# One gated DeltaNet layer on one core: instruction order from a timeline model, with the last products in written order

## The chip, the cores and the metric

The kernel runs on one core of one Trainium2 chip. The metric is device time in microseconds (us) of one execution. The time before is the median of three executions; one more execution was profiled, and all rows of the trace below come from that one.

## The reference: what is computed

One decoder layer: adaptive RMSNorm, the gated DeltaNet mixer (16 value heads, 8 key/query heads, head size 128, 1024 tokens), an output projection, a gated residual sum and a last RMSNorm. Cut to what matters:

```python
hdn = rms_norm(x, norm_g) * (1 + scale) + shift            # 1024 x 1024
qkv, z, b, a = split(hdn @ w_in)                           # 32 + 16 column tiles of 128, and 32 columns
q, k, v = split(silu(causal_depthwise_conv(qkv, conv_w)))  # 4 taps
T = inverse(I + strict_lower(beta * k k^T * decay))        # per chunk and head, a triangular solve
for chunk in chunks:                                       # state S per head
    r = v - (k * e^g) S ;  u = T (beta * r)
    o = (q * e^g) S + (q k^T * decay) u ;  S = S * e^g_last + k_dec^T u
o = rms_norm(o) * silu(z)
out = rms_norm(x + gate * (o @ w_out), final_g)
```

## The kernel before

All matrix products run in fp32 split in two parts (`hi` and `lo`); a product is three matmuls: hi·hi, hi·lo, lo·hi. The two value heads that share a key head form a group, so there are eight groups. After a start-up part (lines 357 to 419: x is normalised, turned and modulated) the middle part (lines 928 to 964) runs the groups as a software pipeline. While group g is scanned over its 8 chunks (`scan`, L677), group g+1 is prepared:

- `norms` (L487) builds the decay mask `em`: 16 DVE instructions (L497), then one Exp on ACT over 2048 columns (L499).
- `stage_a` (L534) makes the matrices of the triangular solve, and solves 32x32 blocks on DVE: 31 dependent pairs of instructions, a multiply (L575) and a subtract (L577), here called the solve. The result goes to DRAM and back (L579, then eight loads at L596), is transposed on DVE (L597 to L599) and is merged by TensorE (`levels`, L587, first matmuls L603 and L605).
- `values` (L632) and `proj_kq` (L474) make projections: 24 matmuls of 512 columns each (L459), a copy and a scaling on ACT (L442, L444), three tap additions on DVE (L446), Silu on ACT (L447), then for values a transpose on TensorE (L639). Their weights come by DMA (L139) into three raw buffers, and are split by ACT (L123) and POOL (L124).
- `out_gate` (L667) makes the gate z; `residual_gate` (L781) runs once, beside group 1's scan, and works on DVE at L229.

TensorE's order in the middle part is written out by hand: `drive` (L902) interleaves the generators by costs and delays in ns, such as `D_L0` = 46000, after which a group's `levels` are placed. `early` (L861) starts the output projection (heads 0 to 3) as filler beside the last two groups.

The end (lines 966 to 1013) computes the other output products, heads 4 to 15, in two halves of tokens (`tg`), each with eight PSUM accumulators of 512 columns: first a loop over heads 4 to 12, then for each of four row tiles the heads 13 to 15, the residual sum on DVE (L847, L848), the sum of squares on ACT (L1012) and `finish` (L986: power on POOL, scaling, store).

What sets the order: the program is traced in written order and then ordered by a scheduler of the framework, which replays it on a model of the machine. On each engine, and on the queue of SP that issues nearly all DMAs, it puts next the instruction that is first in written order among those that are ready at that moment of the model. Every engine then runs its list strictly in that order, waiting where an input isn't there yet. Inside a `tc.manual_schedule(engines=...)` block, the named engines keep the written order instead. Before the change, TensorE is named in the middle part, four engines in most of the start-up part, and DVE alone in the last loop of the end.

Of the kernel before, what the change touches and what calls it, by code (L numbers as in the profile page):

```python
# [17 lines left out]
P = 128  # L18
EPS = 1e-6
# [14 lines left out]
EARLY, NLAST = 4, 3  # L34
# [13 lines left out]
def gdn_layer(ctx: ExitStack, tc: tile.TileContext, x, c, ada_w, ada_b, norm_g, w_in, conv_w, a_log, dt_bias,  # L48
# [8 lines left out]
    nc = tc.nc  # L57
    B, T, D = x.shape
# [3 lines left out]
    HV = 16  # L62
    NTAP = conv_w.shape[1]
    TH = 512
# [17 lines left out]
    neg_half = const.tile([P, 8], F32, name="neg_half")  # L82
# [39 lines left out]
    def split(raw, hi, lo):  # L122
        nc.scalar.copy(hi, raw)  # L123
        nc.gpsimd.tensor_tensor(lo, raw, hi.bitcast(F32), op=ALU.subtract)  # L124
# [27 lines left out]
    banks = ["pj", "pj", "ks", "oq", "ts", "pot"]  # L152

    def bank(tag, shape=(P, TH)):
        return pp.tile(list(shape), F32, name=tag, tag=tag, bufs=nbuf.get(tag, 1))
# [267 lines left out]
    cp = ctx.enter_context(tc.tile_pool(name="cp", bufs=2))  # L423
# [253 lines left out]
    def scan(gi, G):  # L677
# [47 lines left out]
        for n in range(NT):  # L725
# [4 lines left out]
            while len(late) > LAG:  # L730
                if can_finish():
                    finish(*late.pop(0))
                yield 0, 400
            pks = bank("ks", (P, 2, 2, P))
            if n > 0:
                nc.tensor.matmul(pks[:, 0], lhsT=kq[:, 0, js], rhs=st, start=True, stop=True)  # L736
                r = cp.tile([P, 2, P], F32, name="r", tag="r", bufs=1)
                for h in range(2):
                    nc.vector.scalar_tensor_tensor(r[:, h], pks[:, 0, h], negc[:, n, h0 + h:h0 + h + 1], vtok[:, j, h],
                                                   op0=ALU.mult, op1=ALU.add)  # L740
                second(*pend)
                if len(late) > 2 and can_finish():
                    finish(*late.pop(0))
                if n < NT - 1:
                    sg = cp.tile([P, 2, P], F32, name="sg", tag="sg", bufs=1)
                    nc.gpsimd.tensor_tensor(sg, st, gle[:, n, hs, None].to_broadcast([P, 2, P]), op=ALU.mult)
                yield 860, D_R
            else:
                r = vtok[:, 0]
# [26 lines left out]
        while late:  # L776
            if can_finish():
                finish(*late.pop(0))
            yield 215, D_F
# [25 lines left out]
    def load_wo(kt, hf, hl):  # L805

        whi, wlo = hl
        raw = wpool.tile([P, TH], F32, name="woraw", tag="wraw", bufs=3)
        nc.sync.dma_start(out=raw, in_=w_out[kt * P:(kt + 1) * P, hf * TH:(hf + 1) * TH])
        nc.scalar.copy(whi, raw)  # L810
        (nc.vector if kt % 2 else nc.gpsimd).tensor_tensor(wlo, raw, whi.bitcast(F32), op=ALU.subtract)
        return whi, wlo

    def load_wo2(kt):
        hl = [wpool.tile([P, D], F32R, name=n, tag=t, bufs=2) for n, t in (("wohi", "whi"), ("wolo", "wlo"))]
        ww = []
        for hf in range(2):
            s = slice(hf * TH, (hf + 1) * TH)
            raw = wpool.tile([P, TH], F32, name="woraw", tag="wraw", bufs=3)
            nc.sync.dma_start(out=raw, in_=w_out[kt * P:(kt + 1) * P, s])  # L820
            split(raw, hl[0][:, s], hl[1][:, s])
            ww.append((hl[0][:, s], hl[1][:, s]))
        return ww

    def load_g(kt, tg, hl, pool=cp, tag="vT", bufs=2):
        src = pool.tile([P, TH], F32, name="gsrc", tag=tag, bufs=bufs)
        nc.sync.dma_start(out=src, in_=o_dram[kt, :, tg * TH:(tg + 1) * TH])
        ghi, glo = hl
        nc.scalar.copy(ghi, src)
        nc.vector.tensor_tensor(glo, src, ghi.bitcast(F32), op=ALU.subtract)  # L830
        return ghi, glo

    def out_product(acc, t, gw, ww, first, last):
        (ghi, glo), (whi, wlo) = gw, ww
        ts = slice(t * P, (t + 1) * P)
        for n, (a, b) in enumerate(((ghi, whi), (ghi, wlo), (glo, whi))):
            nc.tensor.matmul(acc, lhsT=a[:, ts], rhs=b, start=(first and n == 0), stop=(last and n == 2))  # L837

    wos, gos, rows32 = [], [], []
    rows_of = lambda tg, t: slice((tg * 4 + t) * P, (tg * 4 + t + 1) * P)  # L840
    xrs = {}
    running = []

    def gated_add(acc, yt, tg, t, hf):

        s = slice(hf * TH, (hf + 1) * TH)
        nc.vector.tensor_tensor(yt[:, s], acc, gate_b[:, s], op=ALU.mult)  # L847
        nc.vector.tensor_tensor(yt[:, s], yt[:, s], xrs[tg, t][:, s], op=ALU.add)  # L848
# [114 lines left out]
        for _ in tail:  # L963
            pass

    gate_b, fg = rows32[:2]
    nc.sync.dma_start(out=fg, in_=final_g[None, :].to_broadcast([P, D]))
    banks = ["pj", "pj", "tr", "tr", "ks", "oq", "ts", "pot"]
    last = range(HV - NLAST, HV)
    wlast = None  # L970
    for tg in range(2):
        acc = [[bank(banks[2 * t + hf]) for hf in range(2)] for t in range(4)]
        for kt in range(EARLY, HV - NLAST):
            ww = load_wo2(kt)
            gw = load_g(kt, tg, [cp.tile([P, TH], F32R, name=n, tag=t, bufs=b)
                                 for n, t, b in (("ghi", "ktok", 4), ("glo", "vtok", 3))])
            for t in range(4):
                for hf in range(2):
                    out_product(acc[t][hf], t, gw, ww[hf], kt == EARLY, False)
        if wlast is None:  # L980
            wos += [[cp.tile([P, TH], F32R, name=n, tag=t, bufs=b)
                        for n, t, b in (("wohi", "sz", 2), ("wolo", ("pn2", "tb")[hf], 1))] for hf in range(1)]
            wlast = [[load_wo(kt, hf, wos[2 * i + hf]) for hf in range(2)] for i, kt in enumerate(last)]
        glast = [load_g(kt, tg, gos[i]) for i, kt in enumerate(last)]

        def finish(rs, yt, ss, end):  # L986
            nc.vector.tensor_scalar(ss[:, 0:1], ss[:, 0:1], ss[:, 1:2], EPS, op0=ALU.add, op1=ALU.add)
            nc.gpsimd.tensor_tensor(ss[:, 0:1], ss[:, 0:1], neg_half[:, :1], op=ALU.pow)
            for hf in range(2):
                s = slice(hf * TH, (hf + 1) * TH)  # L990
                if end:
                    nc.vector.scalar_tensor_tensor(yt[:, s], yt[:, s], ss[:, 0:1], fg[:, s], op0=ALU.mult,
                                                   op1=ALU.mult)
                else:
                    nc.scalar.mul(yt[:, s], yt[:, s], ss[:, 0:1])
                    nc.gpsimd.tensor_tensor(yt[:, s], yt[:, s], fg[:, s], op=ALU.mult)
                nc.sync.dma_start(out=out[0, rs, s], in_=yt[:, s])

        with tc.manual_schedule(engines={nc.vector.engine}):
            for t in range(4):  # L1000
                if tg == 0:
                    yt = cp.tile([P, D], F32, name="yt", tag=("at", "at", "ua", "at")[t], bufs=(2, 2, 1, 2)[t])
                else:
                    yt = xrs[0, t]
                ss = cp.tile([P, 2], F32, name="ss", tag="ssk", bufs=2)
                xr = xrs[tg, t]
                for hf in range(2):
                    for i, kt in enumerate(last):
                        out_product(acc[t][hf], t, glast[i], wlast[i][hf], False, i == NLAST - 1)
                    gated_add(acc[t][hf], yt, tg, t, hf)  # L1010
                    s = slice(hf * TH, (hf + 1) * TH)
                    nc.scalar.activation(xr[:, s], yt[:, s], AF.Square, scale=D ** -0.5, accum_out=ss[:, hf:hf + 1])  # L1012
                finish(rows_of(tg, t), yt, ss, t == 3)


_INS = ["x", "c", "ada_w", "ada_b", "norm_g", "gdn_w_in", "gdn_conv_w", "gdn_a_log", "gdn_dt_bias", "gdn_norm_w",
# [19 lines left out]
```

## Time and profile before

| | us |
|---|---|
| median of three executions | 1133.0 (1131.27 to 1133.68) |
| the profiled execution, own time | 1130.95 |
| its span, first to last instruction | 1129.2 |
| TensorE busy in it (share of span) | 1059.3 (94%) |
| VectorE (DVE) | 745.1 (66%) |
| ScalarE (ACT) | 536.6 (48%) |
| GpSimd (POOL) | 450.0 (40%) |
| mean granted TensorE clock | 0.979 |

How to read it: the profiled execution is 2.05 us shorter than the median, and its span is 1.75 us shorter than its own time. A matmul's end in the trace is modelled, so TensorE's gaps are read rather than its busy time. Granted clock is a share of full speed: 1.00 is 2.4 GHz, 0.5 is 1.2 GHz.

### The profile page before, as it was taken

What the parts mean: (1) busy time and instruction counts of PE and PEld (TensorE: products, weight loads), DVE (VectorE), ACT (ScalarE), POOL (GpSimd) and SP (SyncE); (2) the same over time, 40 slices, a digit from 0 to 9 for tenths busy, and PEclk for the clock granted to TensorE, in tenths of its full rate; (3) what the DMA queues carried; (4) which work ended last, traced back from release to release, by engine and by line L of the source; (5) the groups of instructions that cost most, each with busy time, mean ns of one, the idle gap of its engine ahead of it and who ended that gap; (6) DMA issues with size and microseconds to landing.
All of it is one profiled execution on the core that took longest, in us unless ns stands there. A gap on an engine that the chain in (4) does not pass through costs nothing.

```text
span 1129.2 us, 18338 instructions
## 1 busy us (share of the span) xinstructions
PE 1059.3 (94%) x6295; PEld 857.6 (76%) x6295; DVE 745.1 (66%) x1914; ACT 536.6 (48%) x1416; POOL 450.0 (40%) x532
## 2 busy tenths in 40 slices
PE   8997999989999799999999999999899989999997
PEld 7875787767878678777877887788678768778785
DVE  5468775776579857865786677677766866513515
ACT  6567442453642455435543644364546424534523
POOL 3452223532444135323532452155216334954643
PEclk9998999999999999999999999999999989999999
DMA  9803333341145313421531143125313571446442
GB/s 287 234 19 133 75 82 85 101 126 43 39 135 164 83 50 100 125 56 30 145 102 45 42 146 84 39 54 163 74 29 103 149 219 63 140 135 185 152 121 75
DMA packets 188131, 119.48 MB, mean 106 GB/s; under 512 B 59733, under 2 KB 166534, under 8 KB 187014
## 3 DMA queue, kind: packets, MB, share of 16 engines
q1 hardware_dynamic: 187536, 118.20, 37.2%
q8 instruction: 50, 0.82, 0.3%
q14 instruction: 43, 0.35, 0.1%
q10 hardware_dynamic: 502, 0.10, 0.0%
HBM read 93.03 MB, written 25.24 MB: 105 GB/s over the span
## 4 chain that ended last, share of the span: by engine, by line
PE 41%; DVE 18%; ACT 6%; POOL 5%; DMA 4%; issue 4%; SPq 0%; POOLq 0%; DVEq 0%; ACTq 0%
PE pj L459 16%; PE pj L837 5%; DVE tb L577 4%; DVE tm L575 4%; DVE vT L446 3%; DVE em L497 3%; PE tr L549 2%; PE tr L837 2%; PE ts L755 2%; PE ks L736 1%; PE oq L709 1%; PE oq L762 1%; PE tr L622 1%; PE ks L767 1%; PE tr L628 1%
## 5 line engine op out<-in xcount | busy, mean ns | idle before, releaser
L124 POOL TENSOR_TENSOR wlo<-wraw,whi 128x512 fp32r<-128x512 f32 x92 | 126.1, 1379 | 147.3 <-ACT whi L123 107.7
L446 DVE SCALAR_TENSOR_TENSOR vT<-xb,taps,vT 128x512 f32<-128x512 f32 x96 | 84.6, 882 | 24.3 <-ACT vT L444 23.3
L446 DVE SCALAR_TENSOR_TENSOR kq<-xb,taps,kq 128x512 f32<-128x512 f32 x96 | 78.7, 828 | 12.9 <-ACT kq L444 11.0
L123 ACT CAST whi<-wraw 128x512 fp32r<-128x512 f32 x92 | 55.5, 618 | 64.9 <-PE pj L459 59.0
L577 DVE TENSOR_TENSOR tb<-tb,tm 128x126 f32<-128x126 f32 (+22 forms) x248 | 80.1, 323 | 4.8
L698 POOL TENSOR_TENSOR oT<-oT,z 128x256 f32<-128x256 f32 x64 | 50.6, 792 | 81.2 <-ACT oT L697 74.0
L575 DVE TENSOR_TENSOR tm<-tb,ua 128x126 f32<-128x126 f32 (+22 forms) x248 | 78.3, 316 | 6.2 <-DMA ua<-D 1.1
L459 PE MATMUL pj<-h1hia,whi 128*128 128x512 f32 x184 | 75.8, 412 | 6.6 <-ACT vT L444 6.6
L697 ACT ACTIVATE oT<-pot,cols 128x256 f32<-128x256 f32 x64 | 30.4, 474 | 108.1 <-PE pot L695 54.8
L459 PE MATMUL pj<-h0lob,whi 128*128 128x512 f32 x184 | 78.2, 425 | 0.0
L459 PE MATMUL pj<-h0hia,whi 128*128 128x512 f32 x184 | 76.8, 417 | 1.3 <-ACT kq L444 1.3
L459 PE MATMUL pj<-h1hib,whi 128*128 128x512 f32 x184 | 77.8, 423 | 0.0
L459 PE MATMUL pj<-h1lob,whi 128*128 128x512 f32 x184 | 77.7, 422 | 0.0
L459 PE MATMUL pj<-h1hia,wlo 128*128 128x512 f32 x184 | 77.5, 421 | 0.0
L459 PE MATMUL pj<-h0hib,wlo 128*128 128x512 f32 x184 | 77.1, 419 | 0.0
L459 PE MATMUL pj<-h1hib,wlo 128*128 128x512 f32 x184 | 76.6, 416 | 0.0
L459 PE MATMUL pj<-h0hia,wlo 128*128 128x512 f32 x184 | 75.8, 412 | 0.0
L459 PE MATMUL pj<-h1loa,whi 128*128 128x512 f32 x184 | 75.7, 411 | 0.0
L459 PE MATMUL pj<-h0loa,whi 128*128 128x512 f32 x184 | 75.6, 411 | 0.0
L459 PE MATMUL pj<-h0hib,whi 128*128 128x512 f32 x184 | 75.5, 410 | 0.0
L439 POOL MEMSET xb<- 128x3 f32 x32 | 3.4, 109 | 172.3 <-DVE kq L446 85.9
L719 POOL TENSOR_TENSOR sso<-sso,neg_half 128x2 f32<-128x2 f32 x64 | 44.6, 696 | 58.3 <-DVE sso L718 57.6
(445 smaller groups left out, 2933.1 us busy)
## 6 DMA issues: line engine op xcount, KB each, us to landing
wraw<-in_gdn_w_in SPq DMA_DIRECT2D x92, 256.0 KB, 2.9
woraw<-in_gdn_w_out SPq DMA_DIRECT2D x54, 256.0 KB, 3.2
wa<-in_ada_w SPq DMA_DIRECT2D x16, 512.0 KB, 6.9
em<-gc_dram SPq DMA_DIRECT2D x8, 1024.0 KB, 6.4
z_dram<-sz SPq DMA_DIRECT2D x32, 256.0 KB, 2.1
z<-z_dram SPq DMA_DIRECT2D x64, 128.0 KB, 2.4
o_dram<-oT SPq DMA_DIRECT2D x64, 128.0 KB, 1.9
gsrc<-o_dram SPq DMA_DIRECT2D x32, 256.0 KB, 2.9
```

Source lines behind the costliest of these rows:

```text
L123: nc.scalar.copy(hi, raw)
L124: nc.gpsimd.tensor_tensor(lo, raw, hi.bitcast(F32), op=ALU.subtract)
L446: nc.vector.scalar_tensor_tensor(dst, xb[:, j:j + TH], tp[:, j], dst, op0=ALU.mult, op1=ALU.add)
L459: nc.tensor.matmul(ps[:m], lhsT=a[:, k, :m], rhs=b[half][k // 4][:, k % 4], start=(k == 0 and n == 0), stop=(k == KT - 1 and n == 2))
L497: nc.vector.scalar_tensor_tensor(em[:, h, n], em[:, h, n], ngc[:, n, h0 + h:h0 + h + 1], mask, op0=ALU.add, op1=ALU.add)
L549: nc.tensor.matmul(pg2[:, 0:2], lhsT=kq[hf][:, 0, js], rhs=kq[hf][:, :, js], start=True, stop=True)
L575: nc.vector.tensor_tensor(tmv, tb[:, :mm, j:j + 1].to_broadcast([P, mm, ln]), ua[:, j:j + 1, j + 1:].to_broadcast([P, mm, ln]), op=ALU.mult)
L577: nc.vector.tensor_tensor(tb[:, :mm, j + 1:], tb[:, :mm, j + 1:], tmv, op=ALU.subtract)
L697: nc.scalar.mul(oT, pot, normw_c)
L698: nc.gpsimd.tensor_tensor(oT, oT, zs.pop(n), op=ALU.mult)
L719: nc.gpsimd.tensor_tensor(sso, sso, neg_half[:, :2], op=ALU.pow)
L837: nc.tensor.matmul(acc, lhsT=a[:, ts], rhs=b, start=(first and n == 0), stop=(last and n == 2))
```

## The change

Two edits. The context is opened with `schedule_with_timeline_sim=True`: the scheduler replays the program on its timeline model, no longer on its default one, and so may order DVE, ACT, POOL and SP anew wherever no block names them. And the whole end is put in a block that names TensorE, with TensorE added to the inner block that names DVE. Lines 966 to 1013 are otherwise only indented one level deeper; no instruction is added or removed, and no buffer or constant changes.

```diff
-    gate_b, fg = rows32[:2]
+    with tc.manual_schedule(engines={nc.tensor.engine}):
+        gate_b, fg = rows32[:2]
...
-        with tc.manual_schedule(engines={nc.vector.engine}):
-            for t in range(4):
+            with tc.manual_schedule(engines={nc.tensor.engine, nc.vector.engine}):
+                for t in range(4):
...
-    with tile.TileContext(nc) as tc:
+    with tile.TileContext(nc, schedule_with_timeline_sim=True) as tc:
         gdn_layer(tc, *args)
```

## Rows read from the trace of the kernel before

**Rows 1.** The page: busy time of each engine, its share of the span, instructions.
```profile
PE 1059.3 (94%) x6295; PEld 857.6 (76%) x6295; DVE 745.1 (66%) x1914; ACT 536.6 (48%) x1416; POOL 450.0 (40%) x532
```

**Rows 2.** Windows: start:end, length, busy by engine (instructions), granted clock, DMA share, GB/s.
```profile
90.00:125.00 35.00, 27.65 (x105) 21.00 (x103) 28.87 (x87) 26.23 (x59) 9.62 (x8) 0.85 0.35 113
240.00:255.00 15.00, 11.02 (x44) 8.61 (x43) 9.63 (x27) 9.10 (x12) 4.02 (x8) 0.89 0.48 105
364.00:392.00 28.00, 22.00 (x162) 17.01 (x161) 24.32 (x62) 12.29 (x17) 4.32 (x8) 0.94 0.40 96
...
474.00:500.00 26.00, 22.07 (x151) 16.61 (x150) 18.08 (x34) 13.66 (x20) 6.61 (x9) 0.95 0.29 61
...
898.00:926.00 28.00, 21.23 (x82) 15.37 (x81) 20.30 (x46) 6.67 (x11) 9.36 (x8) 0.88 0.67 207
...
1121.00:1129.00 8.00, 0.06 (x1) 0.00 (x0) 3.77 (x6) 2.23 (x6) 3.49 (x3) 0.77 0.42 157
```

**Rows 3.** Timeline near 244 us: ACT, then TensorE (in brackets: idle before, releaser).
```profile
239.89 1.28 ACT L499 ACT_TABLE_LOAD   x1
244.76 1.91 ACT L499 ACTIVATE em<-em 128x2048 f32<-128x2048 f32 x1 [3.59 <-DVE em L497]
...
248.25 0.66 PE L695 MATMUL pot<-ident,o 128*128 128x128 f32 x2 [3.98 <-ACT oT L697]
```

**Rows 4.** Timeline near 367 us: DVE, then TensorE.
```profile
367.06 0.34 DVE L229 SCALAR_TENSOR_TENSOR accg<-wag,cols,accg 128x128 f32<-128x128 f32 x1
...
368.38 0.74 DVE L446 SCALAR_TENSOR_TENSOR vT<-xb,taps,vT 128x512 f32<-128x512 f32 x1
...
369.84 0.66 PE L639 MATMUL tr<-ident,vT 128*128 128x128 f32 x4 [2.62 <-ACT vT L447]
```

**Rows 5.** SP's queue: its longest wait in total, then the timeline of two groups.
```profile
SPq L139 <- POOL wlo L124: 300.5, 71, 17.2
...
162.08 1.29 SPq L579 DMA_DIRECT2D D<-tb  x2
...
165.80 3.79 SPq L596 DMA_DIRECT2D TT<-D  x8
...
475.92 1.27 SPq L579 DMA_DIRECT2D D<-tb  x2
480.12 2.08 SPq L139 DMA_DIRECT2D wraw<-in_gdn_w_in  x2
482.30 3.90 SPq L596 DMA_DIRECT2D TT<-D  x8
```

**Rows 6.** One group's solve: window, then timeline of DVE and TensorE.
```profile
448.00:476.00 28.00, 28.00 (x135) 22.92 (x134) 26.38 (x89) 10.51 (x25) 8.59 (x12) 1.00 0.45 138
...
448.70 0.19 DVE L575 TENSOR_TENSOR tm<-tb,ua 128x31 f32<-128x31 f32 x1
...
488.49 0.44 DVE L599 STREAM_TRANSPOSE TE<-TT 32x256 f32<-32x256 f32 x1
...
492.11 0.21 PE L603 MATMUL tr<-TE,at 32*32 32x32 f32 x1
```

**Rows 7.** Timeline near 235 us: the solve on DVE, and POOL.
```profile
235.19 0.25 DVE L577 TENSOR_TENSOR tb<-tb,tm 128x91 f32<-128x91 f32 x1
235.48 1.35 DVE L575 TENSOR_TENSOR tm<-tb,ua 128x78 f32<-128x78 f32 x1
...
235.44 2.55 POOL L124 TENSOR_TENSOR wlo<-wraw,whi 128x512 fp32r<-128x512 f32 x2 [0.98 <-ACT whi L123]
```

**Rows 8.** The last scan's end: window of L837 alone, then TensorE's timeline.
```profile
980.70:989.70 9.00, 5.61 (x19) 3.24 (x18) 1.00 0.35 102
...
989.58 0.44 PE L695 MATMUL pot<-ident,o 128*128 128x128 f32 x2 [0.89 <-POOL o L720]
...
996.72 0.40 PE L837 MATMUL pj<-wohi,ghi 128*128 128x512 f32 x1
...
1002.21 0.39 PE L837 MATMUL pj<-wohi,ghi 128*128 128x512 f32 x1
```

More of the change, by code (lines that the diff above doesn't have):

```diff
@@ L964, in gdn_layer @@
             pass
-    gate_b, fg = rows32[:2]
[L967 to L976, printed above, removed]
-            for t in range(4):
-                for hf in range(2):
[L979 to L997, printed above, removed]
-        with tc.manual_schedule(engines={nc.vector.engine}):
[L1000 to L1010, printed above, removed]
-                    s = slice(hf * TH, (hf + 1) * TH)
-                    nc.scalar.activation(xr[:, s], yt[:, s], AF.Square, scale=D ** -0.5, accum_out=ss[:, hf:hf + 1])
-                finish(rows_of(tg, t), yt, ss, t == 3)
@@ new lines, in gdn_layer, with finish @@
+    with tc.manual_schedule(engines={nc.tensor.engine}):
+        gate_b, fg = rows32[:2]
+        nc.sync.dma_start(out=fg, in_=final_g[None, :].to_broadcast([P, D]))
+        banks = ["pj", "pj", "tr", "tr", "ks", "oq", "ts", "pot"]
+        last = range(HV - NLAST, HV)
+        wlast = None
+        for tg in range(2):
+            acc = [[bank(banks[2 * t + hf]) for hf in range(2)] for t in range(4)]
+            for kt in range(EARLY, HV - NLAST):
+                ww = load_wo2(kt)
+                gw = load_g(kt, tg, [cp.tile([P, TH], F32R, name=n, tag=t, bufs=b)
+                                     for n, t, b in (("ghi", "ktok", 4), ("glo", "vtok", 3))])
+                for t in range(4):
+                    for hf in range(2):
+                        out_product(acc[t][hf], t, gw, ww[hf], kt == EARLY, False)
+            if wlast is None:
+                wos += [[cp.tile([P, TH], F32R, name=n, tag=t, bufs=b)
+                            for n, t, b in (("wohi", "sz", 2), ("wolo", ("pn2", "tb")[hf], 1))] for hf in range(1)]
+                wlast = [[load_wo(kt, hf, wos[2 * i + hf]) for hf in range(2)] for i, kt in enumerate(last)]
+            glast = [load_g(kt, tg, gos[i]) for i, kt in enumerate(last)]
+            def finish(rs, yt, ss, end):
+                nc.vector.tensor_scalar(ss[:, 0:1], ss[:, 0:1], ss[:, 1:2], EPS, op0=ALU.add, op1=ALU.add)
+                nc.gpsimd.tensor_tensor(ss[:, 0:1], ss[:, 0:1], neg_half[:, :1], op=ALU.pow)
+                for hf in range(2):
+                    s = slice(hf * TH, (hf + 1) * TH)
+                    if end:
+                        nc.vector.scalar_tensor_tensor(yt[:, s], yt[:, s], ss[:, 0:1], fg[:, s], op0=ALU.mult,
+                                                       op1=ALU.mult)
+                    else:
+                        nc.scalar.mul(yt[:, s], yt[:, s], ss[:, 0:1])
+                        nc.gpsimd.tensor_tensor(yt[:, s], yt[:, s], fg[:, s], op=ALU.mult)
+                    nc.sync.dma_start(out=out[0, rs, s], in_=yt[:, s])
+            with tc.manual_schedule(engines={nc.tensor.engine, nc.vector.engine}):
+                for t in range(4):
+                    if tg == 0:
+                        yt = cp.tile([P, D], F32, name="yt", tag=("at", "at", "ua", "at")[t], bufs=(2, 2, 1, 2)[t])
+                    else:
+                        yt = xrs[0, t]
+                    ss = cp.tile([P, 2], F32, name="ss", tag="ssk", bufs=2)
+                    xr = xrs[tg, t]
+                    for hf in range(2):
+                        for i, kt in enumerate(last):
+                            out_product(acc[t][hf], t, glast[i], wlast[i][hf], False, i == NLAST - 1)
+                        gated_add(acc[t][hf], yt, tg, t, hf)
+                        s = slice(hf * TH, (hf + 1) * TH)
+                        nc.scalar.activation(xr[:, s], yt[:, s], AF.Square, scale=D ** -0.5, accum_out=ss[:, hf:hf + 1])
+                    finish(rows_of(tg, t), yt, ss, t == 3)
```

## Prediction

> **What bounds the kernel now.** I read the page first, then the windows by stage, then what TensorE waits for in the stages that lose time, then the queues ahead of those waits.
>
> The page shows TensorE busy 94% of the span and DVE next at 66% [rows 1]. No instruction is added or removed, so the work stays, and 1129.2 - 1059.3 = 70 us of idle TensorE, with what a lowered clock costs beside it, is all that an order can win. The windows say where it lies [rows 2]. Lost in a stretch is its length less TensorE's busy time, plus the missing share of the clock times the length (a small overcount, since part of the slow time is idle):
>
> - 90 to 125: 7.35 idle, 0.15 x 35 = 5.25 by the clock, 12.6 us
> - 240 to 255: 3.98 and 1.65, 5.6 us
> - 364 to 392: 6.0 and 1.7, 7.7 us
> - 898 to 926: 6.8 and 3.4, 10.1 us
> - 474 to 500: 3.9 and 1.3, 5.2 us; three more groups repeat this stretch with 4.0 to 4.1 idle and 0 to 0.8 by the clock
> - 1121 to 1129: 8 us after the last product.
>
> So one part of the loss sits in four places of their own, 36.0 us together, and one part repeats, about 18 us. The clock falls right behind the idle times: 0.89 and 0.94 are the means of windows in which TensorE ran part of the time at 1.2 GHz instead of 2.4.
>
> Two of the four places are plainly matters of order. Near 244 us ACT had loaded the table for the Exp of L499 at 239.9 and then stood 3.59 us until DVE had the last pieces of `em`; behind it in ACT's list stood the scaling L697 for which TensorE waited 3.98 us [rows 3]. Near 367 us DVE ran the residual gate's additions (L229, 0.34 each) ahead of the last tap addition (L446, 0.74) of a tile on which TensorE waited 2.62 us [rows 4]. Both say that the model which made the list held an input ready earlier, or an engine free earlier, than the chip did. SP's queue says the same: weight loads (L139) stood 71 times for POOL's split, 300.5 us in total [rows 5]. What is behind such a load waits too: in the group at 476 us the solve's result was stored from 475.92 and fetched from 482.30, 6.4 us later, with a waiting weight load between; in the first group the same two were 3.7 us apart [rows 5].
>
> **The change, part by part.**
>
> *The order of DVE, ACT, POOL and SP.* It moves any of some 1914 + 1416 + 532 instructions and nearly all DMAs; TensorE's list in the middle part is written out and stays. The trace can't show the new lists, so I bound them. No loss less than zero: if all four places close and half of the repeating loss goes, the gain is 36 + 9 = 45 us. The other end is the rival below, a cost of 20 us. I take this value: the two places with a named misfit close (5.6 + 7.7), and half of 898 to 926 (5.1), where loads for the output weights are queued among others. Nothing for 90 to 125, where DVE is busy 28.9 of 35 us and ACT 26.2 [rows 2], so that there is little else to put first. Nothing for the repeating part, whose waits are of 0.7 to 1.7 us each, about the length of one vector instruction that can't be broken off. That is a gain of 18.4 us. A new list has misfits of its own; I charge one stall of the size of the one at 244 us, 5.6.
>
> *The end in written order.* In the trace 18 products of the end ran on TensorE before the last transposes of the last scan (the window has 18 weight loads; its 19th product is an earlier one's overlap), filling the scan's waits [rows 8]. A product takes 5.49 / 24 = 0.229 us there: the same accumulator is reached again 24 products later, at 996.72 and 1002.21 [rows 8]. If written order also holds them behind the whole middle part, 18 x 0.229 = 4.1 us of filling is gone; the scan's own chain of small steps ends little sooner, as TensorE still stood 0.89 us before its last transpose [rows 8]. If the block orders only its own members, the cost is 0. I leave a gain out: an accumulator that comes again after just one round of 24 products is the written order already. I take 4.1, since the whole end stands behind the middle part in written order. What hid the scan's tail was just these products; `early`'s are used up by then. The last 8 us (residual, norm and stores behind the last product, [rows 2]) keep their order on DVE and stay.
>
> *Sum.* Own time 1130.95 - 18.4 + 5.6 + 4.1 = 1122.25. The median stands 2.05 above the profiled execution, so 1124.3.
>
> **A rule that speaks against it.** A vector instruction of the solve took 1.35 us where its neighbour took 0.25, while POOL ran two weight splits from 235.44 on [rows 7]: 1.1 us lost for one that met a split. In the stretch of one solve, 448 to 476 us, only two of the 128 splits of the kernel run now. If a new order put four more there, the solve would end 4.4 us later, which is the rival below. The Trainium skill, page "SBUF — State Buffer", section "SBUF: two separate sides", has a rule for this: VectorE and GpSimd share a port pair under an exclusive lock, held for a whole instruction, and a vector instruction with two SBUF inputs is blocked by a GpSimd one that reads SBUF. The trace agrees. By that rule a model without the lock would not see what such a placement costs, and the sum would be that of the rival.
>
> **The rivals.**
>
> *Slower: the solve comes too late.* The solve is the one long chain off TensorE with little slack: DVE works from 448.70, its results are transposed by 488.49 + 0.44, and TensorE's first `levels` matmul, placed by hand, came at 492.11 [rows 6]: 3.2 us of slack. Three more groups have 3.1 to 3.2, the one ahead of them 3.8. DVE is busy 26.4 of 28 us in the stretch, with 89 instructions of which 62 are the solve's [rows 6], so each vector instruction that a new order puts between its pairs delays it in full: five tap additions of 0.74 [rows 4] make 3.7 us and use it up. From there on each us costs one in each of five groups, and a stall lowers the clock (1.65 us at the place near 244). Two us past the slack cost 5 x (2 + 1.65) = 18 us; with half of the 8.7 won net in the forecast it gives 1133 - 4.4 + 18 = 1147, and I reckon 1136 to 1156. For it: greedy orders fill a chain's pauses, and in the present list they do. Against it: the solve stands early in written order, so it wins where it is ready, and a quicker fetch on SP (3.7 against 6.4 us) would give 2.7 us of slack back.
>
> *No difference.* TensorE is the bound and its list stays; the present waits may only move from one instruction to the next, the won 18.4 us against as many new. 1131 to 1135. In this I count that the two models order alike, so that the change does nothing but hold back the end's products (1133 + 4.1 would then be the time, 1137, and belongs to slower).
>
> *A larger gain.* The repeating part goes too, and the end costs nothing: 36 to 45 us, 1088 to 1104.
>
> **How the numbers follow.** Forecast 0.52, with a range of its own from 1105 (three places closed and part of the fourth, no costs) to 1130. Slower by the solve 0.22, by the end alone or by other misfits 0.07. No difference 0.14. Larger gain 0.05. About 0.2%, 2.3 us, is what a measurement of this kernel can tell from no change. So faster 0.57, same 0.14, slower 0.29. The range 1102 to 1151 leaves out most of the larger gain and the upper end of the slow case.
>
> **What would show it.** Right: near 244 us the Exp's table load stands behind the last L497, and TensorE no longer waits 4 us for L697; near 367 us L446 stands ahead of L229; the fetch at L596 follows the store at L579 by about 4 us; SP's wait of L139 for POOL falls well under 300 us; and the 18 products stand behind the last transposes, with TensorE idle some 4 to 5 us more between 975 and 990. Wrong: TensorE waits at L603 or L605 for DVE's L599 or for the fetch in several groups (the slow rival), or the solve's stretch holds more than 89 vector instructions; or the list of the start-up's end (90 to 125), from which I expect nothing, moves by more than 4 us.

## The result, and the profile after

| | before | after |
|---|---|---|
| median of the timed executions | 1132.85 us (1131.27 to 1133.68) | 1152.47 us (1150.13 to 1153.85) |
| ratio, 95% interval | 1 | 1.0173 (1.0151 to 1.0194) |
| profiled execution, own time (span) | 1130.95 us (1129.2) | 1150.13 us (1148.4) |
| mean granted clock of TensorE | 0.979 | 0.971 |

The change makes the kernel 19.6 us slower. The forecast was 1124 us, the chance of "slower" was put at 0.29, and the time lies 1.5 us above the range. One of ten executions of a kernel further down (the first of the experiments) took 1474.12 us at a granted clock of 0.65, where the other nine took 1136 to 1149 us; it is left out of its median and ratio.

The page of after, the line of busy times (it answers [rows 1]):

```profile
PE 1065.0 (93%) x6295; PEld 861.1 (75%) x6295; DVE 756.9 (66%) x1914; ACT 536.8 (47%) x1414; POOL 451.4 (39%) x532
```

TensorE runs the same 6295 matmuls, 5.7 us longer in all, and stands idle 83.4 us instead of 70. ACT has 1414 instructions instead of 1416: with its new order it loads a function table 19 times instead of 21. Since TensorE's list is nearly the same in both kernels (at some 230 of the 6295 places it has another line), the two traces can be laid side by side matmul by matmul: how much later the same-numbered matmul starts in after. That table is worked out from the two traces:

```
matmul no.       100    300   1100   1300   2000   2100   2900   4700   5200   5800   6250
starts before   20.5   55.5  207.2  256.4  374.9  385.8  513.2  819.7  899.1 1004.3 1110.6 (us)
after, later by  1.9   14.1   17.9   15.2   15.6   22.0   17.9   13.6   15.1   19.2   19.2 (us)
```

It is to be read by its steps. 14.1 us are lost by 55 us, in the start-up, which no line of the prediction looks at. Another 3.9 come by 207 us, the gates below. The whole group loop, on which the prediction spent most of its words, comes out 4.3 us ahead between matmuls 1100 and 4700, although it holds one loss of 6.4. The last group and the end lose 5.6.

**The start-up.** SP's queue, kernel before and then after (start us, length, queue, line, tiles, count):

```profile
12.70 6.47 SPq L334 DMA_DIRECT2D w0raw<-in_gdn_w_in  x3
19.21 11.16 SPq L219 DMA_DIRECT2D wa<-in_ada_w  x6
30.41 3.25 SPq L139 DMA_DIRECT2D wraw<-in_gdn_w_in  x3
```

```profile
8.59 11.93 SPq L219 DMA_DIRECT2D wa<-in_ada_w  x6
20.56 1.74 SPq L139 DMA_DIRECT2D wraw<-in_gdn_w_in  x1
22.43 0.78 SPq L334 DMA_DIRECT2D w0raw<-in_gdn_w_in  x1
...
29.42 0.76 SPq L334 DMA_DIRECT2D w0raw<-in_gdn_w_in  x1
```

The block around the start-up names TensorE, DVE, ACT and POOL, not SP. So the new model was free to put SP's transfers in another order, and it put four more `wa` and one `wraw` ahead of the first `w0raw`, the weights of the first projection. The code suggests why: `w0raw` takes buffers of the tag `xt`, all eight of which hold x at first, so it is ready only when a tile of x has been used, while `wa` and `wraw` have three buffers each of their own. Exactly three `wa` tiles (six transfers) and three `wraw` went ahead of the last `w0raw`. A model that holds x's buffers busy for longer than the chip does, which could start `w0raw` at 12.70 us, would order them so; the model's own times are not on record, so this is not shown. The first work with those weights, on DVE in the kernel before, then on ACT, DVE and TensorE in after:

```profile
22.23 1.23 DVE L343 TENSOR_TENSOR w<-w0raw,w 128x1024 fp32r<-128x1024 f32 x1 [0.21 <-ACT w L338]
```

```profile
30.27 1.05 ACT L338 CAST w<-w0raw 128x1024 fp32r<-128x1024 f32 x1 [10.43 <-DMA w0raw<-in_gdn_w_in]
31.35 1.23 DVE L343 TENSOR_TENSOR w<-w0raw,w 128x1024 fp32r<-128x1024 f32 x1 [7.39 <-ACT w L338]
36.13 0.69 PE L353 MATMUL ts<-h0hia,w 128*64 128x512 f32 x1 [5.02 <-ACT h0hia L262]
```

L343 starts 9.1 us later. ACT, whose written order has the three copies of `w0raw` (L338) ahead of `h0hia` (L262), stood 10.43 us for the transfer, so TensorE got `h0hia` late. The windows of 20 to 60 us, before and then after (columns as in [rows 2]), hold the price:

```profile
20.00:40.00 20.00, 19.95 (x120) 18.66 (x118) 8.36 (x19) 7.96 (x12) 3.82 (x3) 0.74 1.06 262
40.00:60.00 20.00, 19.68 (x109) 15.86 (x109) 13.72 (x37) 13.62 (x20) 12.88 (x11) 1.00 0.73 193
```

```profile
20.00:40.00 20.00, 13.39 (x82) 11.49 (x83) 7.10 (x13) 5.17 (x7) 2.89 (x3) 0.75 0.91 227
40.00:60.00 20.00, 19.82 (x81) 17.32 (x81) 6.62 (x19) 7.05 (x10) 5.12 (x4) 0.57 0.39 106
```

TensorE is idle 6.6 us longer up to 40 us. Then it is busy 19.82 of 20 us and runs 81 matmuls where it ran 109, since the granted clock is 0.57: most of that window at 1.2 GHz, 0.43 x 20 = 8.6 us. The wait and the clock behind it make 15.2, against a lag of 14.1.

**The gates.** DVE between 77 and 109 us in after: the chain of the gate steps (L298, seven L300, L304, then `gh` at L309), on which TensorE's L310 waits. The first two lines are from the kernel before.

```profile
77.18 0.30 DVE L298 TENSOR_SCALAR gt<-gt 128x128 f32<-128x128 f32 x1
...
86.94 0.28 DVE L309 COPY gh<-gt 128x128 f32<-128x128 f32 x1
```

```profile
93.57 0.87 DVE L298 TENSOR_SCALAR gt<-gt 128x128 f32<-128x128 f32 x1
...
97.25 0.28 DVE L300 SCALAR_TENSOR_TENSOR gt<-gt 128x128 f32<-128x128 f32 x1
97.46 2.07 DVE L446 SCALAR_TENSOR_TENSOR kq<-xb,taps,kq 128x512 f32<-128x512 f32 x3
99.44 0.28 DVE L300 SCALAR_TENSOR_TENSOR gt<-gt 128x128 f32<-128x128 f32 x1
99.64 0.61 DVE L229 SCALAR_TENSOR_TENSOR accg<-wag,cols,accg 128x128 f32<-128x128 f32 x2
100.17 1.41 DVE L446 SCALAR_TENSOR_TENSOR kq<-xb,taps,kq 128x512 f32<-128x512 f32 x2
...
109.04 0.28 DVE L309 COPY gh<-gt 128x128 f32<-128x128 f32 x1
109.47 0.77 PE L310 MATMUL ts<-triu,gh 128*128 128x128 f32 x2 [7.64 <-DVE gh L309]
```

From L298 to L309 it takes 15.5 us. In the kernel before it took 9.8 (77.18 to 86.94), and TensorE did not wait for `gh`. The chain's steps are short, 0.28 us; the list filled each pause behind one with tap additions (0.74 each) and pieces of the residual gate. The block around the gates names TensorE and DVE, but it orders only its own members: instructions written elsewhere may stand between them.

**The loop.** Of TensorE's waits in after (total us, times, longest) two are new or much grown in the loop (the first was 4.0 us, once, in the kernel before):

```profile
PE pot L695 <- ACT oT L697: 9.8, 6, 2.0
...
PE tr L603 <- DVE TE L597: 5.3, 1, 5.3
```

Gone, or cut to 0.5 us in all, are the waits for `vT`, of which [rows 4] show one: 6.6 us at L459 and 6.0 at L639 in the kernel before. Grown is the wait for the scan's state (L736 for DVE's L771), 6.2 us instead of 1.9. SP's longest wait (it answers [rows 5]) and the solve of the group that [rows 6] show, in after:

```profile
SPq L139 <- POOL wlo L124: 228.2, 60, 17.1
```

```profile
465.80 0.19 DVE L575 TENSOR_TENSOR tm<-tb,ua 128x31 f32<-128x31 f32 x1 [1.44 <-DMA ua<-D]
500.80 0.18 DVE L577 TENSOR_TENSOR tb<-tb,tm 128x16 f32<-128x16 f32 x1
501.01 1.27 SPq L579 DMA_DIRECT2D D<-tb  x2
504.56 3.79 SPq L596 DMA_DIRECT2D TT<-D  x8
...
507.95 0.43 DVE L599 STREAM_TRANSPOSE TE<-TT 32x256 f32<-32x256 f32 x1
513.37 0.21 PE L603 MATMUL tr<-TE,at 32*32 32x32 f32 x1
```

The solve lasts 35.2 us instead of 27.2, but its result is fetched 3.6 us behind the store instead of 6.4 and transposed 2.8 us sooner behind that, and it starts 47.6 us ahead of TensorE's hand-placed L603 instead of 43.4. So L603 has 5.0 us of slack where it had 3.2. In one group only this did not hold, that of the residual gate, where the solve lasts 46.3 us (347.5 to 393.8) instead of 32.8:

```profile
393.97 1.26 SPq L579 DMA_DIRECT2D D<-tb  x2
...
400.42 0.42 DVE L597 STREAM_TRANSPOSE TE<-TT 32x256 f32<-32x256 f32 x1
400.90 0.31 PE L603 MATMUL tr<-TE,at 32*32 32x32 f32 x2 [5.34 <-DVE TE L597]
```

### The profile page after: what moved, and what is told of

Same layout as the page of the kernel before. It is cut to its first block, busy times and chain, and to the rows that moved or that the text cites. A ratio compares the mean times of both kernels' runs of the same rounds, so it can differ in the third digit from the quotient of the medians.

```text
span 1148.4 us, 18282 instructions
## 1 busy us (share of the span) xinstructions
PE 1065.0 (93%) x6295; PEld 861.1 (75%) x6295; DVE 756.9 (66%) x1914; ACT 536.8 (47%) x1414; POOL 451.4 (39%) x532
## 5 line engine op out<-in xcount | busy, mean ns | idle before, releaser
L124 POOL TENSOR_TENSOR wlo<-wraw,whi 128x512 fp32r<-128x512 f32 x92 | 119.4, 1316 | 113.6 <-ACT whi L123 103.7
L575 DVE TENSOR_TENSOR tm<-tb,ua 128x126 f32<-128x126 f32 (+22 forms) x248 | 81.0, 327 | 23.3 <-DMA ua<-D 18.0
L446 DVE SCALAR_TENSOR_TENSOR kq<-xb,taps,kq 128x512 f32<-128x512 f32 x96 | 80.9, 848 | 16.7 <-ACT kq L444 14.8
L698 POOL TENSOR_TENSOR oT<-oT,z 128x256 f32<-128x256 f32 x64 | 53.7, 840 | 96.9 <-ACT oT L697 96.9
L123 ACT CAST whi<-wraw 128x512 fp32r<-128x512 f32 x92 | 52.6, 618 | 61.4 <-PE pj L459 53.9
L446 DVE SCALAR_TENSOR_TENSOR vT<-xb,taps,vT 128x512 f32<-128x512 f32 x96 | 76.2, 794 | 6.4 <-ACT vT L444 5.4
L459 PE MATMUL pj<-h0lob,whi 128*128 128x512 f32 x184 | 77.7, 422 | 0.0
L459 PE MATMUL pj<-h0hia,whi 128*128 128x512 f32 x184 | 76.2, 414 | 1.3 <-ACT kq L444 1.3
L459 PE MATMUL pj<-h1hia,wlo 128*128 128x512 f32 x184 | 77.4, 421 | 0.0
L459 PE MATMUL pj<-h1hib,whi 128*128 128x512 f32 x184 | 77.0, 419 | 0.0
L459 PE MATMUL pj<-h1lob,whi 128*128 128x512 f32 x184 | 77.0, 418 | 0.0
L459 PE MATMUL pj<-h0hib,wlo 128*128 128x512 f32 x184 | 76.7, 417 | 0.0
L459 PE MATMUL pj<-h1hib,wlo 128*128 128x512 f32 x184 | 76.4, 415 | 0.0
L459 PE MATMUL pj<-h1loa,whi 128*128 128x512 f32 x184 | 76.0, 413 | 0.0
L459 PE MATMUL pj<-h0hia,wlo 128*128 128x512 f32 x184 | 75.8, 412 | 0.0
L459 PE MATMUL pj<-h0loa,whi 128*128 128x512 f32 x184 | 75.6, 411 | 0.0
L459 PE MATMUL pj<-h1hia,whi 128*128 128x512 f32 x184 | 75.5, 411 | 0.0
L459 PE MATMUL pj<-h0hib,whi 128*128 128x512 f32 x184 | 74.9, 407 | 0.0
```

Source lines behind the costliest of these rows:

```text
L446: nc.vector.scalar_tensor_tensor(dst, xb[:, j:j + TH], tp[:, j], dst, op0=ALU.mult, op1=ALU.add)
L459: nc.tensor.matmul(ps[:m], lhsT=a[:, k, :m], rhs=b[half][k // 4][:, k % 4], start=(k == 0 and n == 0), stop=(k == KT - 1 and n == 2))
L575: nc.vector.tensor_tensor(tmv, tb[:, :mm, j:j + 1].to_broadcast([P, mm, ln]), ua[:, j:j + 1, j + 1:].to_broadcast([P, mm, ln]), op=ALU.mult)
L698: nc.gpsimd.tensor_tensor(oT, oT, zs.pop(n), op=ALU.mult)
```

## The experiments

All ratios are to the kernel before, measured side by side with it on one chip, with 95% intervals. 1 per cent is 11.3 us. Differences in us are taken from the ratios, which differ from the quotients of the medians by up to 0.0014. The kernel before had medians of 1129.2 to 1131.9 us beside the experiments. The changed kernel itself, measured a second time (below), had a ratio of 1.0139 instead of 1.0173, so kernels that were not measured side by side compare to some 4 us only.

**The start-up's transfers.** One word is added to the changed kernel:

```
-    with tc.manual_schedule(engines={nc.tensor.engine, nc.vector.engine, nc.scalar.engine, nc.gpsimd.engine}):
+    with tc.manual_schedule(engines={nc.tensor.engine, nc.vector.engine, nc.scalar.engine, nc.gpsimd.engine, nc.sync.engine}):
```

> The changed kernel with one word added: SP joins the engines that keep their written order in the start-up block. Theory A (the loss is made in the first 70 us, because SP's transfers of the start-up were put in another order and the first projection weights landed 9 us late): the copy of w0raw waits until about 22 us instead of 31, TensorE's idle 5.02 us at 31.11 goes, its busy time between 25 and 50 us rises from 19.0 to 24 us or more, and 14 of the 21.5 us lost come back: 1138 us, 1135 to 1142. Theory B (the loss is the prediction's second case, the triangular solve too late in the group loop; the start-up's lag is slack that is made up elsewhere): 1149 to 1155 us.

Measured: 1146.34 us, ratio 1.0117 (1.0087 to 1.0147). That is some 6 us back (1.0173 - 1.0117; 2.5 against the second measurement), not 14. TensorE's idle time at 31 us is gone and the lag at matmul 300 is 3.3 us instead of 14.1. At matmul 1100 the lag is 11.9 us: 8.5 are lost since in this execution, twice what after lost there. Part of it is the clock: from 160 to 210 us TensorE was as busy as in after (48.80 and 48.64 us), at a granted clock of 0.90 instead of 1.00. The time lies between the two theories, nearer to B.

The other way round, the kernel before with its start-up transfers in the order that the change gave them:

```
...
-        for j in range(3):
-            first_w(j, True)
         for i in (1, 2):
             ada_load(i)
+        for j, (c0, k4) in enumerate(((9 * P, 0), (9 * P, 4), (P, 0))):
+            early_raw.append(wraw_load(c0, k4, P))
+            first_w(j, True)
```

(The lines left out name SP in the block, so that it keeps written order, and let `load_w` take the pieces loaded here.)

> The kernel before, under its own scheduler, with SP's start-up transfers written in the order that the change gave them: x, six transfers of wa, then wraw and w0raw by turns. Theory A: it loses what the changed kernel lost there, about 14 us: 1147 us, 1143 to 1151, with TensorE waiting near 31 us. Theory B: 1131 to 1135 us, as the kernel before.

Measured: 1143.46 us, ratio 1.0095 (1.0058 to 1.0132), 10.8 us slower. Its first matmul of the projections (timeline; the lines stand five lower in this file), then its windows:

```profile
36.11 0.69 PE L358 MATMUL ts<-h0hia,w 128*64 128x512 f32 x1 [5.45 <-ACT h0hia L267]
```

```profile
20.00:40.00 20.00, 13.59 (x73) 11.89 (x72) 5.03 (x10) 5.16 (x7) 2.54 (x2) 0.68 0.89 225
40.00:60.00 20.00, 19.82 (x94) 16.57 (x94) 9.44 (x27) 9.52 (x14) 6.12 (x5) 0.73 0.49 136
```

The same wait at the same place, and the same low clock behind it, with nothing else of the change in the kernel. The lag is 11.02 us at matmul 300 and 11.02 at matmul 1100. So the order of SP's start-up transfers alone costs this kernel about 11 us. The last 3 of the 14 are within what executions differ there: the two kernels below whose start-up is untouched (the end block alone, the residual gate spread) stand 2.9 and 3.2 us behind the profile of before at matmul 300, and two more with the late start-up of after (the changed kernel without its end block, and with the residual gate spread) only 11.0 and 8.7.

Which transfers? A third kernel holds SP to written order among the first 17 transfers only:

```
+        with tc.manual_schedule(engines={nc.sync.engine}):
             for t in range(NT):
                 x_load(t)
...
             for j in range(3):
                 first_w(j, True)
             for i in (1, 2):
                 ada_load(i)
```

It was timed beside the changed kernel itself.

> The changed kernel as it is, on the chip of the three that follow, as their reference: 1.015 to 1.019 of the kernel before.

> The changed kernel with SP held to written order among 17 transfers alone (x, the first wa, the three w0raw, then two more wa); three wraw, which are written later, slip in ahead of w0raw. Ahead of the second w0raw lie 6.75 MB instead of 8.5 in the changed kernel and 6 in the kernel before. At the 260 GB/s that SP's queue moved there the copy of w0raw should wait until about 25 us (31.35 in the changed kernel, 22.23 before). Theory A, now with the size that the first runs showed for the whole start-up order (6 to 11 us): 5 to 9 us come back against the changed kernel of the same call. Rival: the later wa transfers, not w0raw, make the start-up's loss: less than 3 us comes back.

Measured: the changed kernel 1148.57 us, ratio 1.0139 (1.0102 to 1.0176), a little under what was expected; the one with the first weights ahead 1139.29 us, ratio 1.0065 (1.0038 to 1.0091). 8.4 us come back, in the expected 5 to 9. SP's queue there (timeline), then the windows:

```profile
12.38 4.71 SPq L139 DMA_DIRECT2D wraw<-in_gdn_w_in  x3
17.22 4.28 SPq L334 DMA_DIRECT2D w0raw<-in_gdn_w_in  x3
```

```profile
20.00:40.00 20.00, 19.06 (x124) 17.44 (x125) 9.27 (x20) 6.96 (x10) 3.04 (x4) 0.84 0.97 239
40.00:60.00 20.00, 19.43 (x108) 15.58 (x108) 13.74 (x38) 13.79 (x21) 12.94 (x11) 0.99 0.77 207
```

Three `wraw` are still ahead of `w0raw`, and L343 starts at 24.63 us, 2.4 later than before. What that costs can't be told from nothing: the lag at matmul 300 is 1.0 us here, and 3.0 and 4.2 in the two later traces with this order, where an untouched start-up showed up to 3.2. A delay of 2.4 us was bridged, one of 9.1 was not. The order of `w0raw` against the later `wa` is what matters.

**The gates.** In the next kernel `gh` is copied ahead of the step's end, and the first convolutions are written into the same ordered block behind it, so that they can't lie inside the chain:

```
...
+        nc.vector.tensor_copy(gh.rearrange("p (h n) -> p n h", n=NT), v3(g))
         yield 0, D_G
...
-    with tc.manual_schedule(engines=GENG):
-        next(gate_steps)
-        drain(len(units))
+    gate_block = ExitStack()
+    gate_block.enter_context(tc.manual_schedule(engines=GENG))
+    next(gate_steps)
+    drain(len(units))
...
             cv(acc0[j][hf], kq0[hf][:, j], tag="vtok", bufs=3)
+    gate_block.close()
```

With SP's whole start-up in written order:

> The kernel with SP's start-up in written order (theory A above), and the gate chain on VectorE kept together: the copy gh is written ahead of the step's end, and the first convolutions are written into the same ordered block behind it, so that they cannot lie between the dependent gate steps. Theory A: TensorE's idle 7.64 us at 101.82 (L310 <- DVE gh) falls to under 3, and another 4 to 5 us come back: 1134 us, 1131 to 1137. Rival: the gates' wait is made up in the next group, where TensorE has slack: 1136 to 1141 us, as with SP's order alone.

Measured: 1136.9 us, ratio 1.0026 (1.0001 to 1.0051), against 1.0117 without the gate edit on the same chip: 10 us, twice what was expected. Alone, with SP's late order kept:

> The changed kernel with the gate chain kept together on VectorE and nothing else (SP's start-up order stays as the change made it). If the gates' loss is its own (first runs: about 10 us between SP's order alone and SP's order with the gates): 7 to 11 us come back against the changed kernel. If it hangs on the start-up (its trace shows only 4 to 5 us more lag between 70 and 190 us): 3 to 5 us.

Measured: 1146.68 us, ratio 1.0127 (1.0093 to 1.0162), against 1.0139: 1.4 us, within the intervals of both and under either expectation. 10 and 1.4 us don't fit together, so the gates were measured twice more. With the first weights ahead as reference:

> The changed kernel with SP held to written order among the first 17 transfers, as the reference of the next one on the same chip: 1.004 to 1.009 of the kernel before.

> As the run before it, with the gate chain kept together on VectorE. If the gates cost what their traces show (VectorE's chain from L298 to L309 lasts 15.5 us instead of 9.8, and TensorE's lag grows by 4 to 8 us between 70 and 190 us): 3 to 7 us less than the run before it. If they cost nothing by themselves, and the 10 us between the first two kernels with and without them came from the clock: within 2 us of it.

Measured: 1141.41 us, ratio 1.0075 (1.0045 to 1.0105) without, 1133.69 us, ratio 1.0014 (0.9995 to 1.0033) with the gate edit: 6.9 us. And the gates' cost put into the kernel before, by operations without effect in each of the seven steps:

```
         for d in (15, 13, 11, 9, 7, 5, 3):
             nc.vector.scalar_tensor_tensor(q, q, 1.0 / d, s2, op0=ALU.add, op1=ALU.mult)
+            for _ in range(3):
+                nc.vector.tensor_tensor(u, u, u, op=ALU.max)
```

> The kernel before with three operations without effect (128x128, about 0.29 us each) behind each of the seven steps L300 of the gate chain, some 6 us of VectorE in all, so that the chain lasts about 15.5 us as in the changed kernel instead of 9.8. If the gates' chain is on the path: TensorE waits 6 to 8 us for gh and the time rises by 3 to 7 us (1.003 to 1.006). If TensorE has other work there: within 1 us (1.000 to 1.001).

Measured: 1138.66 us, ratio 1.0055 (1.0027 to 1.0083), 6.2 us slower. `gh` comes at 96.02 and the chain lasts 17.7 us from L298 on, 2.2 more than in after, so the 6.2 are rather too many. TensorE waits as it does in after (the lines stand two lower in this file):

```profile
96.43 0.77 PE L312 MATMUL ts<-triu,gh 128*128 128x128 f32 x2 [7.54 <-DVE gh L311]
```

So the gates cost 6 to 10 us where the start-up is in order (10, 6.9 and 6.2). With the late start-up the edit's gain was not told apart from nothing. One part of it stays open: with the gate edit TensorE still waits at the next step, as the convolutions now come later, in the late start-up and in the repaired one alike (here the kernel with first weights and gates, whose lines stand two or three lower):

```profile
102.55 1.11 PE L518 MATMUL tr<-ident,kq 128*128 128x128 f32 x4 [8.22 <-ACT kq L449]
```

In the repaired one its lag is 3.0 us at matmul 300 and 4.5 at 1100 all the same, in the late one 13.6 and 17.3. Why the edit pays in the one and hardly in the other wasn't tried.

**The end.** The kernel before with the second edit alone (the ordered block around the end, no timeline model), and the changed kernel without it. The first differs from the changed kernel by this line, the second from the kernel before by the same line the other way round:

```
-    with tile.TileContext(nc, schedule_with_timeline_sim=True) as tc:
+    with tile.TileContext(nc) as tc:
```

> The kernel before with the second edit alone (the end's products in written order on TensorE, no timeline model). The prediction's step: the 18 products that lay ahead of the last scan's transposes are held behind them and TensorE idles 4 to 5 us more there: 1135 to 1139 us. Theory now: the block orders only its own members against each other, the products stay where they were between the scan's instructions, and the time is that of the kernel before within 2 us: 1131 to 1135 us.

Measured: 1133.87 us, ratio 1.0009 (0.9988 to 1.0029). Theory now, not the prediction's step: 18 products still lie ahead of the last scan's last transposes, as in the kernel before. In after, too, there are 21.

> The changed kernel without its second edit: the timeline model orders all engines, TensorE too where the end is concerned. If the ordered block at the end costs what the changed kernel loses in the last scan's end (2.2 us between 1004 and 1010, where fewer end products lie between the scan's instructions than before), this gives 2 us back against the changed kernel: 1150 us, 1148 to 1152, and the idle times of 0.4 to 0.9 us after L762 go. If the block costs nothing: 1151 to 1154 us. If the model puts the end's products in a worse order, which the block prevents: 1155 us or more.

Measured: 1150.47 us, ratio 1.0185 (1.0159 to 1.0210), the same as with the block (1.0173) within the intervals. Its lag grows by 2.0 us at the end of the last scan, as in after (2.2), though 41 products lie there instead of 21. So no cost of the block shows, though up to 3 us of it would lie within the intervals. Those 2 us stand in every trace of this study with the timeline model and in none without it, so they come with the order of the other engines in the scan's tail. TensorE's waits there in after:

```profile
1004.42 0.71 PE L709 MATMUL oq<-vh,em 128*128 128x128 f32 x4 [0.72 <-ACT o L764]
...
1008.50 0.44 PE L695 MATMUL pot<-ident,o 128*128 128x128 f32 x2 [0.92 <-POOL o L720]
...
1009.55 0.50 PE L837 MATMUL pot<-wohi,ghi 128*128 128x512 f32 x1 [0.61 <-ACT oT L697]
```

**The one long wait of the loop.** The residual gate's eight pieces lie in the group of the late solve. They are spread over four groups, two in each:

```
...
-            if gi == RG:
-                streams.append(residual_gate())
+            if RG <= gi < RG + 4:
+                streams.append(residual_gate(2 * (gi - RG), 2 * (gi - RG) + 2))
```

(The lines left out let `residual_gate` take the range of its pieces.) Behind start-up and gates, with the end block and without it, then on the changed kernel and on the kernel before:

> As e5 (SP's start-up in written order, the gate chain kept together), and the eight pieces of the residual gate are spread over four groups, two in each, instead of all eight in the group that holds TensorE's one long idle time in the loop (5.37 us at 383.47 in e5, L605 <- DVE TE). Theory C: there the solve lasts 46.3 us instead of 35.2 since some 40 instructions of the residual gate lie in it; with two pieces in each group it lasts about 38, the idle time falls under 1 us, no other group gets one, and 4 to 5 us come back: 1131 to 1133 us where e5 gave 1136.9 (ratio to before 0.997 to 1.000). Rival: the solve is late there for its loads (ua waits for a transfer), the idle time stays over 3 us and the time that of e5.

> As e6 without the second edit, so that TensorE at the end is ordered by the model. If the block costs 2 us: 1129 to 1131 us, the fastest of all (ratio to before 0.996 to 0.999). If not: as e6 or slower.

> The changed kernel with the residual gate's pieces spread over four groups and nothing else. The idle time of 5.34 us at 395.56 (L603 <- DVE TE) goes. If it is the price of the longer solve: 4 to 8 us come back. The kernel before gained 9 us from the same edit without having that idle time, so if the gain is the spread's own, and the solve costs nothing beyond it, it is the same 9 us here, and if the model's order gives it back in the later groups, as it did behind the start-up and gates edits, under 3.

> The kernel before, with its own scheduler, and the residual gate's eight pieces spread over four groups. Its solve lasts 32.8 us in that group and 27.0 in the others, and its idle time of 2.62 us at 367 (L639 <- ACT vT) lies in the same group. Theory: that idle time goes and little else, 1.5 to 3 us: ratio 0.997 to 0.999. If the kernel before has slack there: 1.000.

Measured: 1139.61 us, ratio 1.0090 (1.0072 to 1.0108); 1138.12 us, 1.0072 (1.0055 to 1.0088); 1152.11 us, 1.0172 (1.0144 to 1.0200); and, for the kernel before with the spread, 1120.9 us, 0.9918 (0.9901 to 0.9934).

In all three kernels with the timeline model the wait at L603 is gone. So the residual gate is what made that solve too late. But none of them gains (1.0172 against 1.0139 on the same chip; 1.0090 against 1.0026 of the kernel without the spread on another), and theory C falls in that half: on the changed kernel the lag drops from 15.4 to 10.1 us between matmuls 2000 and 2900, and is back at 16.7 by 4700. On the changed kernel three of the four groups that now hold two pieces have a solve of 38 us, and TensorE waits longer for the scan's state than in after (6.2 us, 9 times), as its longest waits show:

```profile
PE pot L695 <- ACT oT L697: 10.1, 6, 2.0
PE ks L736 <- DVE st L771: 9.0, 11, 2.2
```

Under the default order little is given back (the lag is -6.5 us at matmul 6250), and the spread is worth 7 to 11 us: the fastest kernel of this study is the kernel before with this one edit, faster than both. Its lag against before falls from -0.3 to -7.6 us between matmuls 2000 and 2900. The theory had 1.5 to 3 us for it; the single idle time of [rows 4] only shrank, to 1.48, and each of the two groups won 4 to 5 us. In the window of that place [rows 2] TensorE is busy 25.66 us instead of 22.00, and its clock is 1.00 instead of 0.94:

```profile
364.00:392.00 28.00, 25.66 (x223) 19.84 (x221) 21.50 (x35) 10.34 (x19) 8.42 (x11) 1.00 0.30 67
```

That is 5.3 us of the 7.7 that the prediction had counted as lost there. What else in the spread makes the gain was not taken apart.

## Why the prediction was wrong, point by point

**What bounds the kernel** held: TensorE, and idle time with the clock behind it. The step that failed is the bound "No loss less than zero" with one stall of 5.6 us for all that a new order can spoil; behind it stands the list of the places that can move. The prediction took its stretches from where the kernel before lost time, from 90 us on, and asked what an order could win there. TensorE hardly waited in the first 70 us, so they were not looked at. But a free order can lose where nothing was lost. The missing term is the start-up: the block there names four engines, and SP, the fifth, which the change sets free by name, isn't among them. It costs 11 us in the kernel before (10.8), and 8.4 came back in the changed one with the first weights ahead, 2.5 to 6 with all of it in written order. That order could not be known, but its price could: four `wa` of 512 KB and one `wraw` of 256 KB ahead of `w0raw`, 2.36 million bytes, are 9.0 us at the 262 GB/s of its window, and L343 came 9.1 later.

**"Nothing for 90 to 125"** had the wrong bound. The prediction bounded the stretch below by zero because DVE and ACT were busy there, "so that there is little else to put first". It named the sign to look for, a move of more than 4 us, and it came: a wait of 7.64 us for `gh`, and a cost of 6 to 10 us by the runs where the start-up is in order. A busy DVE means that there was other work to put *between* the steps of a chain that TensorE waits for.

**The place near 244 us** is right in its mechanism and half right in its size. ACT's scaling now stands ahead of the Exp's table load, and TensorE waits 1.25 instead of 3.98 us:

```profile
258.85 0.48 ACT L697 ACTIVATE oT<-pot,cols 128x256 f32<-128x256 f32 x1 [3.01 <-PE pot L695]
259.35 1.28 ACT L499 ACT_TABLE_LOAD   x1
...
264.96 0.41 PE L695 MATMUL pot<-ident,o 128*128 128x128 f32 x2 [1.25 <-ACT oT L697]
```

The lag falls by 2.7 us from matmul 1100 to 1300, and by 2.0 to 2.8 in the eight other traces with this loop; 5.6 were forecast. **The place near 367** is half right: the wait of 2.62 us is down to 0.48, at 387 (DVE's list still has L229 and L446 by turns), but the same group got the L603 wait of 5.34. Both lie between matmuls 1300 and 2900, where the lag grows by 2.7 us instead of shrinking by 7.7. **Half of 898 to 926** did not come: the same stretch, 17 us later, is idle 7.7 us with a clock of 0.91, against 6.8 and 0.88 [rows 2]:

```profile
915.00:943.00 28.00, 20.29 (x77) 14.80 (x76) 21.25 (x42) 6.67 (x12) 10.09 (x8) 0.91 0.82 261
```

**Nothing for the repeating part** was too little: from matmul 2900 to 4700 the lag falls by 4.3 us, and by 4.4 to 6.4 in the eight other traces. TensorE's waits for L444, at L639 and behind the solve gave way to one of 1.7 to 2.0 us per group at L695.

**One new misfit, 5.6** was the term that was too small: the start-up and the gates are such misfits too, and cost two to three times as much. That the late solve alone cost 5.34 is luck, since the 5.6 was the size of another stall at another place. The late solve is the first rival's mechanism in one group of seven: DVE's list in that solve holds 20 additions of the residual gate, 7.79 us, where it held 16, 5.96. In the other groups the rival failed: the solve did grow, by 8.0 us in the group shown, more than the 3.2 of slack, but the quicker fetch, which the prediction put against it at 2.7 us, was worth 2.8, the transposes another 2.8, and the solve began 4.2 us earlier against L603. So the slower side came by another mechanism than the one to which most of its chance was given; "other misfits" had 0.07 together with the end.

**The end, 4.1** was wrong. The block orders its own members against each other and holds nothing behind the middle part; this was the prediction's other end, 0. The 2.2 us lost in the scan's tail come with the other engines' order.

**The port rule** had no part in it. In the solve's stretch there are 5 splits where there were 2, but the 31 L575 took 10.08 us against 9.24, and over the whole kernel the mean L575 took 327 ns against 316. An instruction of the solve that meets a split does last longer, by 0.6 us in the mean against its like that meets none; but 30 of the 496 met one in after, and 32 in the kernel before.

**A slip in the prediction's sums:** a larger gain of 36 us would end at 1133 - 36 = 1097, not at 1104. Nothing hangs on it.

The sum, made anew from the runs: with start-up and gates both repaired, the ratio is 1.0026 (1.0001 to 1.0051) or 1.0014 (0.9995 to 1.0033), 3 or 1.6 us. So the two together make 13 to 18 of the 15.7 to 19.6 us that the changed kernel loses by its two measurements. They don't add up as two separate prices: the start-up repaired alone gave 2.5 to 8.4 us back, the gates alone 1.4, and the gates behind a repaired start-up 7 to 10. That part is open. The forecast's gain is in what is left: from matmul 1100 to 4700 the lag falls by 2.6 to 8.7 us in the nine traces with this loop (4.3 in after), the late solve's loss counted in, and behind that 2.6 to 5.6 us are lost again, in the last group and the scan's tail.

## What to carry to other kernels

When a change sets an engine's order free, go through the program by stages and list which queues are pinned in each, the queue that issues transfers among them; here the dearest place was not where time was lost before but where a first operand waited behind megabytes that nobody needed yet. Price such an order as bytes put ahead over the queue's rate, less what TensorE has to bridge it, and count the idle time again for the clock that follows. A filler between the short steps of a chain is free only if nothing waits for the chain's end.

## What the runs showed of the hardware that was not expected

Here the slow clock behind a wait cost more than the wait. In after TensorE was idle 6.6 us between 20 and 40 us, and then, busy 19.82 of 20 us, had a granted clock of 0.57 up to 60 us: 8.6 us. From 33.4 to 57.3 us it stood at the lower level, 0.50, throughout. In the same two windows the clock was 0.74 and 1.00 in the kernel before, 0.68 and 0.73 in it with the late order, and 0.84 and 0.99 with the first weights ahead.

Executions of one kernel spread with the clock that they are granted. The kernel with the first weights ahead took 1130.39 us at a mean clock of 0.983 and 1146.87 at 0.967: 16.5 us for 0.016, where 0.016 of its span is 18. The kernel before, on one chip, took 1128.73 at 0.979 and 1138.35 at 0.969. The changed kernel was granted 0.963 to 0.978 in six executions, the kernel before 0.969 to 0.982 in 25. So a difference of medians here holds the waits and what the clock made of them, and a few executions don't tell 3 us apart.
